# Whole weight splits, issued five steps ahead, and a recurrence that needs no paired PSUM bank

## The chip, the cores and the metric

The kernel runs on one core of one Trainium2 chip. A core has a matrix engine (TensorE, PE in the profile), VectorE (DVE), ScalarE (ACT), GpSimd (POOL) and DMA queues, here issued by SyncE (SP). Each engine works through its own list of instructions in order, and engines wait for each other on semaphores. The time is the device time of one execution, in microseconds (us), as the median of several runs.

## The reference

Two layers are applied to x of 256 tokens by 2048 channels. Each layer normalises x, multiplies it by one combined input projection, runs two groups of heads and adds an output projection. Cut to what matters:

```python
for l in range(DEPTH):                                   # DEPTH = 2
    proj = rms_norm(x, norm_g[l]) @ w_in[l]              # 2048 -> IN_COLS
    rw_in, g_rw, q, k_at, v_at, g_at = split(proj)
    r, k, v, xw, xa = split(bidir_token_shift(rw_in, shift_mu[l]))
    y_rw = rwkv7_branch(r, k, v, xw, xa, ...)            # 16 heads of 64, both directions:
    #   S = S * w_t - (S kk_t) (a_t kk_t)^T + v_t k_t^T ;  y_t = S r_t
    y_at = window_attention(rope(q), rope(k_at), v_at, sink[l])
    x = x + concat(y_rw * silu(g_rw), y_at * silu(g_at)) @ w_out[l]
out = rms_norm(x, final_g)
```

## The kernel before

**Weights.** All weights arrive in halves of 128 x 1024 f32 (512 KB), 280 of them, in three buffers `raw`. Each is split into two tiles: `hi`, a copy rounded by ACT (L215), and `lo = raw - hi` by DVE (L216), in two buffers each. `wsplit` does that in two parts of 512 columns: `hi` part, `lo` part, `hi` part, `lo` part. A half of the weights is then used in eight *steps* of three matmuls of 128 x 256 (L273 `hi` by `XH`, L274 `hi` by `XL`, L275 `lo` by `XH`), which add up in a PSUM bank `pm`. In the output projections the operands are called `MH` and `ML`.

**Order.** `Stream` hands out the steps. It issues the load and the split of the next half as soon as no more than PREFETCH steps of the present one are left (2 before). `window` runs 64 steps in 14 slots, and ahead of each slot's steps it lets generators continue up to their next `yield`. PE's instructions stand exactly in the order of the program; those of the other engines are put in order by a scheduler with priorities, by default the order of the program, with 95 places of preference for `scan_b`.

**The scan.** The recurrent heads go in eight pairs, both directions at once, in four chunks of 64 tokens. Pair p is prepared by `scan_p` in window p+1 (slots in STAGE_P); `scan_i` inverts the chunks' triangular matrices in window p+2 (STAGE_I, its last pieces in slots 0 and 1 of the window after); `scan_b` runs the recurrence over the chunks in window p+3 (STAGE_B, its tail in window p+4). So in windows 4 to 8 of each layer three pairs are in work at once; after window 9 come windows with the last scans and attention, then the output projection, which is matmuls of weights alone.

**Names.** In `scan_i`: `pg` and `ge` are the chunks' products and their masked copy (DVE L724, once for each direction), `AB` a 16-bit copy of a part (ACT L733), `pt` transpositions that ACT copies to `bt` (L754) and, by four copies, to `suv` (L759). `pq`, `pd`, `tv`, `tt` belong to the doubling of the inverse: matmuls L803 and L813 into `pq`, L819 and L821 into `pd`, casts L822 and L823. Its last steps are `pf` (L829 adds a negated identity NEYE times `tv`), `q` (ACT L836), `pn` (L840) and `vf = 2 tt + pn` (DVE L842). In `scan_b`, for each chunk: `r` (L866, in bank `pcc`, or `py` in the first chunk), copied to `rh` by ACT (L869, L872); `pu = vf rh` (L885), copied to `suv` (L890); the state in `pcc` (L888, L895) scaled into the next `suv` (DVE L897); outputs in `py` (L877, L902). Its tail is the last transposition, L922 into `pyt`, with ACT `t` (L924), DVE `t` and `mf` (L925, L614), ACT `MH` (L615) and DVE `ML` (L616).

**PSUM.** `ps_main` holds two banks for `pm`, `ps_c` one bank each for `pcc` and `py`, and `ps_w` two slots of two banks, the paired banks, in which `pg`, `pt`, `pq`, `pd`, `pf`, `pn`, `pu`, `pyt` and others take turns (`wpair`, `wbank`). A matmul into a new tile waits until the last reader of the slot's older tile is done.

Of the kernel before, what the change touches and what calls it, by code (L numbers as in the profile page):

```python
# [21 lines left out]
T = 256  # L22
# [22 lines left out]
STAGE_P = [4, 6, 7, 8, 9, 10, 11, 13]  # L45
STAGE_I = (list(range(SLOTS)), [0, 1])
STAGE_B = (list(range(1, 14)), [3])
# [6 lines left out]
PREFETCH = 2  # L54
# [74 lines left out]
def hybrid_trunk_kernel(ctx, tc, xT, wi, wv, wo, par, fing, dup, iup, sink, pos, cst, out):  # L129
# [21 lines left out]
    def wbank(name):  # L151
        return wpair(name)[:, 0]
# [52 lines left out]
    def wload(src):  # L205
        raw = wrp.tile([128, 1024], F32, tag="raw", name="raw")
        SY.dma_start(out=raw, in_=src)
        return raw

    def wsplit(raw):  # L210
        hi = wsp.tile([128, 1024], F32R, tag="hi", name="hi")
        lo = wsp.tile([128, 1024], F32R, tag="lo", name="lo")
        for i in range(2):
            q = slice(i * 512, (i + 1) * 512)
            A.activation(hi[:, q], raw[:, q], AF.Copy)  # L215
            V.tensor_tensor(lo[:, q], raw[:, q], hi[:, q].bitcast(F32), op=ALU.subtract)  # L216
        return hi, lo

    def halves(src, first=None):
        return [lambda: wsplit(first if first is not None else wload(src[0])), lambda: wsplit(wload(src[1]))]  # L220
# [78 lines left out]
    EYE, NEYE = (cp.tile([128, 64], F16, name=n) for n in ("EYE", "NEYE"))  # L299
# [6 lines left out]
    def setup():  # L306
# [49 lines left out]
        V.tensor_scalar(NEYE, EYE, -1.0, None, op0=ALU.mult)  # L356
        yield
# [248 lines left out]
    def layer(l):  # L606
# [24 lines left out]
        def scan_p(p, t):  # L631
# [21 lines left out]
            pk = wbank("pk")  # L653
            head_sums(pk, sq)
# [3 lines left out]
            for x in (LW[:, 0:T], LW[:, T : 2 * T][:, ::-1]):  # L658
                V.tensor_tensor_scan(x, msk, x, 0.0, op0=ALU.mult, op1=ALU.add)  # L659
            PP = st("pp", [2, NC, 64])  # L660
# [47 lines left out]
        def scan_i(p, t):  # L708
# [129 lines left out]
            pn = wbank("pn")  # L838
            for d, c, h in dch:
                PE.matmul(pn[half[h ^ d], d * T + c * 64 : d * T + (c + 1) * 64], hx(FN, d, c, h), hx(TT, d, c, h), start=True, stop=True)  # L840
            VF = st("vf", [2, NC * 64])
            V.scalar_tensor_tensor(  # L842
                VF.rearrange("p d x -> p (d x)"), TT.rearrange("p d c j -> p (d c j)"), 2.0, pn, op0=ALU.mult, op1=ALU.add
            )
# [3 lines left out]
        def scan_b(p, t):  # L848
# [3 lines left out]
            pc = ps_c.tile([128, 512], F32, tag="c", name="pcc")  # L852
            pS = pc[:, 0:128].rearrange("p (d j) -> p d j", d=2)
            pyt = ps_c.tile([128, 512], F32, tag="y", name="py")
            py = pyt[:, 0:256].rearrange("p (c j) -> p c j", j=64)
            for i in range(NC):
# [3 lines left out]

                pr = [pc[:, 128:192], pc[:, 192:256] if i else pyt[:, 256:320]]
                for d in range(2):
                    for h in range(2):

                        r = half[1 - h] if i == 0 else every
                        PE.matmul(pr[d][half[h ^ d]], GE[h][r, d, ci[d], 0, :], SUV[r, d, ci[d], h, :], start=True, stop=True)  # L866
                RH = st("rh", [2, 64], bufs=2)
                if i:
                    A.activation(RH, pc[:, 128:256].rearrange("p (d j) -> p d j", d=2), AF.Copy)  # L869
                else:  # L870
                    for d in range(2):
                        A.activation(RH[:, d, :], pr[d], AF.Copy)  # L872
# [8 lines left out]
                pu = wpair("pu")  # L881
                for d in range(2):
                    for h in range(2):
                        x = half[h ^ d]
                        PE.matmul(pu[half[h], d, 0:64], t["VF"][x, d, cs(ci[d])], RH[x, d, :], start=True, stop=True)  # L885
# [3 lines left out]
                for h in range(2):  # L889
                    A.activation(here(h), pu[half[h], :, 0:64], AF.Copy)  # L890
# [28 lines left out]
            pz = wbank("pyt")  # L919
# [4 lines left out]
            A.activation(Zt, pz[:, 0:T], AF.Identity, scale=prm(P_LG, p), bias=prm(P_LB, p))  # L924
# [220 lines left out]
```

## Time and profile before

| | |
|---|---|
| median of 3 runs | 1244.04 us (1242.3 to 1247.03) |
| profiled execution, its own time | 1247.3 us |
| its span | 1245.5 us |
| PE busy | 1184.3 us (95%), 16140 matmuls |
| DVE busy | 937.5 us (75%) |
| ACT busy | 739.9 us (59%) |
| DMA queue of the loads | 164.27 MB, 38.5% of 16 engines' span |
| mean granted PE clock | 0.987 |

Of the 16140 matmuls 6720 are those of the weights. A line of a timeline reads: start, duration, engine, line of the kernel, operation, output and input, shape, count, and in brackets the idle time ahead of it with what ended it. Groups by form give total busy time, the mean of one in ns, and the idle time ahead. Matmuls overlap, so what one costs is read from start to start.

### The profile page before, as it was taken

To read this page: it belongs to the slowest core of one execution; us is meant where nothing else is said; L and a number is where in the kernel's file an instruction comes from. 1 tells how busy PE (TensorE), PEld (TensorE's weight loads), DVE (VectorE), ACT (ScalarE), POOL (GpSimd) and SP (SyncE) were. 2 spreads that over 40 slices of the span, in tenths; PEclk is the share of its full clock that TensorE was granted. 3 is DMA by queue.
4 is the path that set the end of the run, shared out by engine and by line. 5 is a ranking of instruction groups with operands and counts; after the bars stand their busy time and mean duration, and the time that the engine had idled before them with its cause. 6 is when DMAs were issued, how large, how long until landed. Compare 5 with 4: busy or idle time off the path is not lost.

```text
span 1245.5 us, 38032 instructions
## 1 busy us (share of the span) xinstructions
PE 1184.3 (95%) x16140; PEld 1092.3 (88%) x16140; DVE 937.5 (75%) x2082; ACT 739.9 (59%) x1838; POOL 19.0 (2%) x23
## 2 busy tenths in 40 slices
PE   6989999999998999999999999999999989999996
PEld 6978888888887989989998888888888888899996
DVE  6878878887976678856666888878887766786654
ACT  6646665766565466645555656665766555675553
POOL 0000000000000000000000000000000000000000
PEclk9999999999999999999999999999999999999998
DMA  7443233322322434466554433233223324435653
GB/s 246 156 143 122 88 116 109 105 93 94 134 77 93 133 109 142 140 204 224 210 182 143 143 110 119 93 111 109 104 93 100 112 99 131 140 130 174 212 190 119
DMA packets 60410, 166.70 MB, mean 134 GB/s; under 512 B 7728, under 2 KB 22736, under 8 KB 60240
## 3 DMA queue, kind: packets, MB, share of 16 engines
q1 hardware_dynamic: 60240, 164.27, 38.5%
q8 instruction: 126, 2.06, 0.7%
q14 instruction: 44, 0.36, 0.1%
HBM read 157.43 MB, written 4.19 MB: 130 GB/s over the span
## 4 chain that ended last, share of the span: by engine, by line
PE 48%; DVE 18%; issue 16%; ACT 11%; DMA 4%; SPq 1%; POOL 0%; DVEq 0%; POOLq 0%; ACTq 0%
PE pm L273 13%; PE pm L275 11%; PE pm L274 11%; DVE lo L216 3%; DMA g<-dup 3%; PE pg L718 2%; DVE kd L665 2%; ACT hi L215 2%; DVE ge L724 2%; ACT AB L733 2%; ACT suv L759 2%; DVE lw L659 2%; ACT ge L771 1%; DMA rrot<-u 1%; ACT bt L754 1%
## 5 line engine op out<-in xcount | busy, mean ns | idle before, releaser
L273 PE MATMUL pm<-XH,hi 128*128 128x256 f32 x1664 | 498.1, 299 | 14.5 <-ACT XH L178 6.1
L275 PE MATMUL pm<-XH,lo 128*128 128x256 f32 x1664 | 471.4, 283 | 11.2 <-DVE lo L216 11.2
L274 PE MATMUL pm<-XL,hi 128*128 128x256 f32 x1664 | 470.6, 283 | 0.1
L215 ACT ACTIVATE hi<-raw 128x512 fp32r<-128x512 f32 x560 | 329.6, 625 | 212.1 <-PE pm L274 170.0
L216 DVE TENSOR_TENSOR lo<-raw,hi 128x512 fp32r<-128x512 f32 x560 | 369.0, 687 | 84.0 <-ACT hi L215 76.7
L273 PEld LDWEIGHTS pm<-XH,hi 128*128 128x128 f32 x1664 | 316.5, 190 | 40.2 <-issue 13.0
L275 PEld LDWEIGHTS pm<-XH,lo 128*128 128x128 f32 x1664 | 316.8, 190 | 14.6 <-DVE lo L216 14.4
L274 PEld LDWEIGHTS pm<-XL,hi 128*128 128x128 f32 x1664 | 317.3, 191 | 0.8 <-DVE XL L179 0.8
L273 PE MATMUL pm<-MH,hi 128*128 128x256 f32 x512 | 145.5, 284 | 2.3 <-ACT hi L215 2.3
L275 PE MATMUL pm<-MH,lo 128*128 128x256 f32 x512 | 145.2, 284 | 0.1
L274 PE MATMUL pm<-ML,hi 128*128 128x256 f32 x512 | 145.0, 283 | 0.0
L273 PEld LDWEIGHTS pm<-MH,hi 128*128 128x128 f32 x512 | 97.9, 191 | 3.2 <-ACT hi L215 2.5
L275 PEld LDWEIGHTS pm<-MH,lo 128*128 128x128 f32 x512 | 97.8, 191 | 0.4 <-DVE lo L216 0.4
L274 PEld LDWEIGHTS pm<-ML,hi 128*128 128x128 f32 x512 | 98.0, 191 | 0.0
L890 ACT ACTIVATE suv<-pu 64x128 f32<-64x128 f32 x128 | 34.5, 270 | 24.8 <-PE pcc L888 13.6
L724 DVE TENSOR_TENSOR ge<-pg,C 128x1024 f32<-128x1024 f32 x32 | 39.1, 1221 | 3.5 <-PE pg L718 3.5
L970 ACT ACTIVATE mv<-mv,mx 128x257 f32<-128x257 f32 x64 | 31.9, 504 | 15.9 <-DVE mx L967 15.9
L733 ACT ACTIVATE AB<-ge 64x512 f16<-64x512 f32 x32 | 20.2, 630 | 34.3 <-DVE ge L724 33.9
L718 PE MATMUL pg<-mv,bk 64*128 64x128 f32 x512 | 37.2, 285 | 0.0
L822 DVE CAST_PREDICATED tv<-LV,pd 128x256 f16<-128x256 uint8 x80 | 34.0, 426 | 4.1 <-PE pd L821 3.7
L815 ACT ACTIVATE QF<-pq 128x256 f16<-128x256 f32 x80 | 30.8, 385 | 6.8 <-PE pq L813 5.5
L823 DVE CAST_PREDICATED tt<-LV,pd 128x256 f16<-128x256 uint8 x80 | 34.0, 425 | 0.0
(241 smaller groups left out, 1833.7 us busy)
## 6 DMA issues: line engine op xcount, KB each, us to landing
raw<-wi SPq DMA_DIRECT2D x207, 512.0 KB, 3.8
raw<-wo SPq DMA_DIRECT2D x64, 512.0 KB, 3.8
raw<-wv SPq DMA_DIRECT2D x8, 512.0 KB, 3.6
rrot<-u SPq DMA_DIRECT2D x80, 32.0 KB, 2.3
vg<-xT SPq DMA_DIRECT2D x16, 128.0 KB, 3.6
xd<-vg SPq DMA_DIRECT2D x16, 128.0 KB, 3.6
vg<-xd SPq DMA_DIRECT2D x16, 128.0 KB, 3.5
g<-dup SPq DMA_DIRECT2D x16, 97.0 KB
```

What stands on the lines that cost most here:

```text
L215: A.activation(hi[:, q], raw[:, q], AF.Copy)
L216: V.tensor_tensor(lo[:, q], raw[:, q], hi[:, q].bitcast(F32), op=ALU.subtract)
L273: PE.matmul(pm, wh, rh[:, kk, :], start=(kk == 0), stop=False)
L274: PE.matmul(pm, wh, rl[:, kk, :], start=False, stop=False)
L275: PE.matmul(pm, wl, rh[:, kk, :], start=False, stop=(kk == 15))
L718: PE.matmul(pg[:, h, c * 128 : (c + 1) * 128], BK[half[h], d, c, 1 - h : 3 - h, :].rearrange("p s j -> p (s j)"), MV[half[h], d, c].rearra ...
L724: V.tensor_tensor(GEd(d), pg.rearrange("p h (c x) -> p h c x", c=NC), gm[d].unsqueeze(1).unsqueeze(1).to_broadcast([128, 2, NC, 128]), op= ...
L733: A.activation(flat(AB[half[h]]), GE[h][half[h]].rearrange("p d c s j -> p (d c) s j")[:, :, 0, :], AF.Copy)
L822: V.copy_predicated(t_sub(TC), t_mask, flat4(pd[:, :, 0:128]))
L823: V.copy_predicated(v_sub(TT), v_mask, flat4(pd[:, 0, 128:384].rearrange("p (d x) -> p d x", d=2)))
L890: A.activation(here(h), pu[half[h], :, 0:64], AF.Copy)
L970: A.activation(Sc[:, h, q, 0:257], Sc[:, h, q, 0:257], AF.Exp, scale=0.125, bias=mx[:, q : q + 1], accum_out=den[:, q : q + 1])
```

## The change

Five things are edited. (1) `wsplit` makes one `hi` and one `lo` of 1024 columns; the very first weight keeps two parts. (2) PREFETCH goes from 2 to 5 steps. (3) STAGE_P gets slot 5, with a further `yield`, so that `pk` is written a slot after the scans of `lw`; the tail of STAGE_B moves from slot 3 to slot 1. (4) The term `2 tt` is added on PE, by four matmuls per pair with EYE2, twice the identity, into `pn`, which becomes a paired bank; ACT copies it to `vf`. Rows are arranged so that `vf` has its input and output on the same half of the partitions. (5) In the recurrence `r`, `u` and the state lie in one bank `pcc`, taken anew for each chunk, so that `pu` takes no paired bank and `rh` is one copy in every chunk; the last transposition goes into the free half of `py`'s bank.

```diff
--- before.py
+++ after.py
@@ -42,16 +42,16 @@
 
 
 SLOTS = 14
-STAGE_P = [4, 6, 7, 8, 9, 10, 11, 13]
+STAGE_P = [4, 5, 6, 7, 8, 9, 10, 11, 13]
 STAGE_I = (list(range(SLOTS)), [0, 1])
-STAGE_B = (list(range(1, 14)), [3])
+STAGE_B = (list(range(1, 14)), [1])
 ATT = [
     [4, 11],
     [1, 3, 6, 8, 11, 13],
     [0, 2, 5, 7, 8, 10, 12, 13],
 ]
 PRIO_B = 95
-PREFETCH = 2
+PREFETCH = 5
 
 
 def _layout():
@@ -207,17 +207,17 @@
         SY.dma_start(out=raw, in_=src)
         return raw
 
-    def wsplit(raw):
+    def wsplit(raw, parts=1):
         hi = wsp.tile([128, 1024], F32R, tag="hi", name="hi")
         lo = wsp.tile([128, 1024], F32R, tag="lo", name="lo")
-        for i in range(2):
-            q = slice(i * 512, (i + 1) * 512)
+        for i in range(parts):
+            q = slice(i * 1024 // parts, (i + 1) * 1024 // parts)
             A.activation(hi[:, q], raw[:, q], AF.Copy)
             V.tensor_tensor(lo[:, q], raw[:, q], hi[:, q].bitcast(F32), op=ALU.subtract)
         return hi, lo
 
     def halves(src, first=None):
-        return [lambda: wsplit(first if first is not None else wload(src[0])), lambda: wsplit(wload(src[1]))]
+        return [lambda: wsplit(first, 2) if first is not None else wsplit(wload(src[0])), lambda: wsplit(wload(src[1]))]
 
     class Stream:
 
@@ -296,7 +296,7 @@
     LV = cp.tile([128, NL, 2, 128], U8, name="LV")
     AB, AL, QF = (cp.tile([128, 2, NC, 64], F16, name=n) for n in ("AB", "AL", "QF"))
     MSK = cp.tile([128, NC, 64], F16, name="MSK")
-    EYE, NEYE = (cp.tile([128, 64], F16, name=n) for n in ("EYE", "NEYE"))
+    EYE, NEYE, EYE2 = (cp.tile([128, 64], F16, name=n) for n in ("EYE", "NEYE", "EYE2"))
     band = cp.tile([128, 512], BF16, name="band")
     FG = cp.tile([128, NKT], F32, name="FG")
     SK = cp.tile([128, DEPTH * 16], F32, name="SK")
@@ -354,6 +354,7 @@
         V.tensor_copy(band, cin[:, 0:512])
         V.tensor_copy(EYE, cin[:, 512 + 64 * NL : 576 + 64 * NL])
         V.tensor_scalar(NEYE, EYE, -1.0, None, op0=ALU.mult)
+        V.tensor_scalar(EYE2, EYE, 2.0, None, op0=ALU.mult)
         yield
 
     def window(n, *gens, groups=SLOTS):
@@ -650,13 +651,14 @@
             KR = st("kkr", [T])
             A.activation(KR, K, AF.Identity, scale=prm(P_KK, p))
             yield
-            pk = wbank("pk")
-            head_sums(pk, sq)
 
             V.tensor_scalar(LW, LW, 1.0, None, op0=ALU.add)
             msk = MSK.rearrange("p c j -> p (c j)")
             for x in (LW[:, 0:T], LW[:, T : 2 * T][:, ::-1]):
                 V.tensor_tensor_scan(x, msk, x, 0.0, op0=ALU.mult, op1=ALU.add)
+            yield
+            pk = wbank("pk")
+            head_sums(pk, sq)
             PP = st("pp", [2, NC, 64])
             IP = st("ip", [2, NC, 64])
             A.activation(PP.rearrange("p d c j -> p (d c j)"), LW, AF.Exp, scale=DECAY_C)
@@ -835,13 +837,17 @@
             FN = st("q16", [2, NC, 64], F16)
             A.activation(FN.rearrange("p d c j -> p d (c j)"), pf[:, :, 0:T], AF.Copy)
             yield
-            pn = wbank("pn")
+
+            pn = wpair("pn")
+            for d in range(2):
+                for h in range(2):
+                    PE.matmul(
+                        pn[half[h], d, 0:T], EYE2[half[h ^ d]], TT[half[h ^ d], d].rearrange("p c j -> p (c j)"), start=True, stop=False, skip_group_check=True
+                    )
             for d, c, h in dch:
-                PE.matmul(pn[half[h ^ d], d * T + c * 64 : d * T + (c + 1) * 64], hx(FN, d, c, h), hx(TT, d, c, h), start=True, stop=True)
+                PE.matmul(pn[half[h], d, cs(c)], hx(FN, d, c, h), hx(TT, d, c, h), start=False, stop=True, skip_group_check=True)
             VF = st("vf", [2, NC * 64])
-            V.scalar_tensor_tensor(
-                VF.rearrange("p d x -> p (d x)"), TT.rearrange("p d c j -> p (d c j)"), 2.0, pn, op0=ALU.mult, op1=ALU.add
-            )
+            A.activation(VF, pn[:, :, 0:T], AF.Copy)
             t["VF"] = VF
             yield
 
@@ -849,27 +855,21 @@
             GE, MV, BT, SUV, PC, bv = (t[n] for n in ("GE", "MV", "BT", "SUV", "PC", "bv"))
 
 
-            pc = ps_c.tile([128, 512], F32, tag="c", name="pcc")
-            pS = pc[:, 0:128].rearrange("p (d j) -> p d j", d=2)
             pyt = ps_c.tile([128, 512], F32, tag="y", name="py")
             py = pyt[:, 0:256].rearrange("p (c j) -> p c j", j=64)
             for i in range(NC):
                 ci = [order[d][i] for d in range(2)]
 
                 here = lambda h, i=i: pick(SUV, half[h], i * 128 + h * 64, [NC * 128 + (NC - 1 - 2 * i) * 128, 2], [1, 64])
-
-                pr = [pc[:, 128:192], pc[:, 192:256] if i else pyt[:, 256:320]]
+                pc = ps_c.tile([128, 3, 2, 64], F32, tag="c", name="pcc")
+                pS = pc[:, 2]
                 for d in range(2):
                     for h in range(2):
 
                         r = half[1 - h] if i == 0 else every
-                        PE.matmul(pr[d][half[h ^ d]], GE[h][r, d, ci[d], 0, :], SUV[r, d, ci[d], h, :], start=True, stop=True)
+                        PE.matmul(pc[half[h], 0, d, :], GE[h][r, d, ci[d], 0, :], SUV[r, d, ci[d], h, :], start=True, stop=True)
                 RH = st("rh", [2, 64], bufs=2)
-                if i:
-                    A.activation(RH, pc[:, 128:256].rearrange("p (d j) -> p d j", d=2), AF.Copy)
-                else:
-                    for d in range(2):
-                        A.activation(RH[:, d, :], pr[d], AF.Copy)
+                A.activation(RH, pc[:, 0], AF.Copy)
                 yield
                 if i > 0:
                     for d in range(2):
@@ -878,16 +878,14 @@
                                 py[half[h], ci[d], :], MV[half[h], d, ci[d], 1, :], SUV[half[h], d, ci[d], h, :],
                                 start=False, stop=False, skip_group_check=True,
                             )
-                pu = wpair("pu")
                 for d in range(2):
                     for h in range(2):
-                        x = half[h ^ d]
-                        PE.matmul(pu[half[h], d, 0:64], t["VF"][x, d, cs(ci[d])], RH[x, d, :], start=True, stop=True)
+                        PE.matmul(pc[half[h], 1, d, :], t["VF"][half[h], d, cs(ci[d])], RH[half[h], d, :], start=True, stop=True)
                 if 0 < i < NC - 1:
                     for h in range(2):
                         PE.matmul(pS[half[h]], ident[half[h], half[h]], here(h), start=True, stop=False, skip_group_check=True)
                 for h in range(2):
-                    A.activation(here(h), pu[half[h], :, 0:64], AF.Copy)
+                    A.activation(here(h), pc[half[h], 1], AF.Copy)
                 yield
                 if i < NC - 1:
                     for d in range(2):
@@ -916,12 +914,12 @@
             yield
             V.tensor_tensor(ysq, py, yv.unsqueeze(2).to_broadcast([128, NC, 64]), op=ALU.mult)
             yield
-            pz = wbank("pyt")
+            pz = pyt[:, T : 2 * T]
             for c in range(NC):
                 for h in range(2):
                     PE.matmul(pz[half[h], cs(c)], ysq[half[h], c, :], ident[half[h], half[h]], start=True, stop=True)
             Zt = st("t1", [T], bufs=3)
-            A.activation(Zt, pz[:, 0:T], AF.Identity, scale=prm(P_LG, p), bias=prm(P_LB, p))
+            A.activation(Zt, pz, AF.Identity, scale=prm(P_LG, p), bias=prm(P_LB, p))
             V.tensor_tensor(Zt, Zt, bv, op=ALU.add)
             mix_split(p, Zt, t["gr"])
             yield
```

The first place is ACT in a steady window, from the last copy of one pair's inverse to the copies of `pt` (slots 0 to 3). Before:

```order
L836 ACTIVATE q_4431<-pf 128x512
L872 ACTIVATE rh<-pcc 128x64
L872 ACTIVATE rh<-py 128x64
L733 ACTIVATE AB<-ge 64x512 x2
L890 ACTIVATE suv<-pu 64x2x64 x2
L771 ACTIVATE ge<-mv 64x6x64
L215 ACTIVATE hi<-raw 128x512
L754 ACTIVATE bt<-pt 128x768
L759 ACTIVATE suv<-pt 64x4x64 x4
L771 ACTIVATE ge<-mv 64x6x64
L924 ACTIVATE t_4588<-pyt,PR 128x256
```

and with the change, in which lines have moved by a few (L922 is `t`, L850 `vf`, L735 `AB`, L888 `suv`, L756 `bt`, L761 the four copies):

```order
L838 ACTIVATE q_4333<-pf 128x512
L922 ACTIVATE t_4377<-py,PR 128x256
L650 ACTIVATE t_4599<-kr,PR 128x256
L850 ACTIVATE vf<-pn 128x512
L872 ACTIVATE rh<-pcc 128x128
L616 ACTIVATE MH<-mf 128x256
L735 ACTIVATE AB<-ge 64x512 x2
L888 ACTIVATE suv<-pcc 64x2x64 x2
L773 ACTIVATE ge<-mv 64x6x64
L215 ACTIVATE hi<-raw 128x1024
L756 ACTIVATE bt<-pt 128x768
L761 ACTIVATE suv<-pt 64x4x64 x4
```

`t` of the tail, `vf` and `MH` now stand ahead of `AB`; `t` stood behind the four copies. There is one `rh` for two.

The second place is DVE in the same stretch. Before:

```order
L724 TENSOR_TENSOR ge<-pg,C 128x2x512
L842 SCALAR_TENSOR_TENSOR vf<-tt,pn 128x512
L784 COPY tt<-EYE 128x512
L724 TENSOR_TENSOR ge<-pg,C 128x2x512
L764 TENSOR_TENSOR AL<-ge,AB 64x512 x2
L808 COPY_PREDICATED tt<-LV,AB 128x128
L216 TENSOR_TENSOR lo<-raw,hi 128x512
L897 TENSOR_TENSOR suv<-pcc,pc 64x2x64 x2
L925 TENSOR_TENSOR t_4588<-t_4588,bv 128x256
L806 COPY_PREDICATED tv<-LV,pq 128x2x128
L614 SCALAR_TENSOR_TENSOR mf<-t_4588,vg 128x256
L809 COPY_PREDICATED tt<-LV,pq 128x128
```

and with the change (L726 is `ge`, L923 `t`, L895 `suv`):

```order
L726 TENSOR_TENSOR ge<-pg,C 128x2x512
L923 TENSOR_TENSOR t_4377<-t_4377,bv 128x256
L786 COPY tt<-EYE 128x512
L615 SCALAR_TENSOR_TENSOR mf<-t_4377,vg 128x256
L617 TENSOR_TENSOR ML<-mf,MH 128x256
L726 TENSOR_TENSOR ge<-pg,C 128x2x512
L766 TENSOR_TENSOR AL<-ge,AB 64x512 x2
L810 COPY_PREDICATED tt<-LV,AB 128x128
L216 TENSOR_TENSOR lo<-raw,hi 128x1024
L895 TENSOR_TENSOR suv<-pcc,pc 64x2x64 x2
L808 COPY_PREDICATED tv<-LV,pq 128x2x128
```

`vf` is gone from DVE; `t`, `mf` and `ML` of the tail stand between the two `ge`.

The third place is DVE around the reciprocal of `kd`, in the middle of the window. Before:

```order
L216 TENSOR_TENSOR lo<-raw,hi 128x512 x2
L897 TENSOR_TENSOR suv<-pcc,pc 64x2x64 x2
L684 TENSOR_TENSOR lw<-lw,kr 128x512
L665 RECIPROCAL kd<-pk 128x256
L399 TENSOR_TENSOR u<-pm,rb 128x256
L666 SCALAR_TENSOR_TENSOR kd<-kd,kkr 128x256
L822 COPY_PREDICATED tv<-LV,pd 128x2x32x4
L401 SCALAR_TENSOR_TENSOR vg<-u,PR,vg 128x255
L823 COPY_PREDICATED tt<-LV,pd 128x2x32x4
L402 SCALAR_TENSOR_TENSOR vg<-u,PR,vg 128x255
```

and with the change (L667 is the reciprocal, L824 and L825 the casts), at the same place:

```order
L686 TENSOR_TENSOR lw<-lw,kr 128x512
L895 TENSOR_TENSOR suv<-pcc,pc 64x2x64 x2
L216 TENSOR_TENSOR lo<-raw,hi 128x1024
L667 RECIPROCAL kd<-pk 128x256
L400 TENSOR_TENSOR u<-pm,rb 128x256
L668 SCALAR_TENSOR_TENSOR kd<-kd,kkr 128x256
L824 COPY_PREDICATED tv<-LV,pd 128x2x32x4
L402 SCALAR_TENSOR_TENSOR vg<-u,PR,vg 128x255
L825 COPY_PREDICATED tt<-LV,pd 128x2x32x4
L403 SCALAR_TENSOR_TENSOR vg<-u,PR,vg 128x255
```

`lw` (L684, now L686) and `suv` stood behind the two parts of `lo`, and stand ahead of the whole one; the order from the reciprocal to the casts is the same.

## The prediction

> **What bounds the kernel now.** I read the page's first part.
>
> ```profile
> PE 1184.3 (95%) x16140; PEld 1092.3 (88%) x16140; DVE 937.5 (75%) x2082; ACT 739.9 (59%) x1838; POOL 19.0 (2%) x23
> ```
>
> TensorE (PE) is busy 95% of the span of 1245.5 us. An edit pays only if PE waits less or works less; time saved on VectorE (DVE) or ScalarE (ACT) pays only where PE is waiting for it. So the next view is PE's waits. The columns are total us, number, longest.
>
> ```profile
> PE pq L803 <- ACT suv L759: 11.6, 12, 1.5
> PE pm L275 <- DVE lo L216: 11.2, 15, 1.6
> ...
> PE pt L741 <- DVE ge L724: 3.0, 2, 1.7
> ...
> PE pf L829 <- DVE tt L823: 1.6, 2, 1.0
> ...
> PE pq L813 <- DVE tv L822: 1.5, 5, 0.4
> PE pq L813 <- DVE tt L823: 0.9, 4, 0.3
> ```
>
> The scan windows in the middle of each layer repeat, so one of the layer's five stands for ten; the columns are the window, its length and the busy time of PE, the weight loads, DVE, ACT and POOL.
>
> ```profile
> 300.32:343.18 42.86, 41.85 (x751) 37.69 (x752) 35.89 (x76) 27.84 (x73) 1.01 (x1) 1.00 0.30 103
> ```
>
> PE is busy 41.85 of 42.86 us. Its one large gap stands at slot 3; in PE's timeline and ACT's, of the window two before this one:
>
> ```profile
> 219.09 0.68 PE L922 MATMUL pyt<-C,ysq 64*64 64x64 f32 x16
> 219.71 0.45 PE L895 MATMUL pcc<-suv,bt 128*64 128x64 f32 x8
> ...
> 221.25 0.33 PE L803 MATMUL pq<-tv,AB 64*64 64x32 f16 x11 [0.86 <-ACT suv L759]
> ```
>
> ```profile
> 215.86 1.28 ACT L733 ACTIVATE AB<-ge 64x512 f16<-64x512 f32 x2 [2.10 <-DVE ge L724]
> 217.17 0.56 ACT L890 ACTIVATE suv<-pu 64x128 f32<-64x128 f32 x2
> 217.75 0.53 ACT L771 ACTIVATE ge<-mv 64x384 f32<-64x384 f32 x1
> ...
> 218.82 0.81 ACT L754 ACTIVATE bt<-pt 128x768 f32<-128x768 f32 x1
> 219.65 1.55 ACT L759 ACTIVATE suv<-pt 64x256 f32<-64x256 f32 x4
> ```
>
> `pq` needs a slot of the paired banks. There are two: `pyt` of L922 has just taken one, and `pt` holds the other until ACT has emptied it, at 221.20.
>
> **The slot-3 wait.** In the change `pu` and `pyt` take no slot, so `pq` goes into one that is free, and the four `suv` copies are next needed by the `pq` of slot 4 (L813 before). The ten steady waits and the two of window 9 make up the 11.6 us row; I count 8.6 in the steady windows (10 x 0.86).
>
> What is late next: the last transposition with its tail (ACT `t`, DVE `t` and `mf`, ACT `MH`, DVE `ML`) now stands at slot 1 ahead of the second `ge` on DVE and of `AB` on ACT, and `vf` goes from DVE to ACT. I replay the queues with rows of the same stretch.
>
> ```profile
> 212.88 0.34 PE L840 MATMUL pn<-tt,q 64*64 64x64 f16 x10
> ```
>
> ```profile
> 213.37 0.69 DVE L842 SCALAR_TENSOR_TENSOR vf<-tt,pn 128x512 f32<-128x512 f16 x1
> ...
> 214.60 1.23 DVE L724 TENSOR_TENSOR ge<-pg,C 128x1024 f32<-128x1024 f32 x1 [0.22 <-PE pg L718]
> ```
>
> ```profile
> L1043 DVE TENSOR_TENSOR mv<-mv 128x1024 f32<-128x1024 f32 x3 | 3.7, 1222 | 0.0
> ...
> L1042 ACT ACTIVATE mv<-X 128x1024 f32<-128x1024 f32 x3 | 3.0, 1048 | 0.0
> ...
> L836 ACT ACTIVATE q<-pf 128x512 f16<-128x512 f32 x16 | 9.3, 580 | 0.3 <-PE pf L834 0.3
> ```
>
> The transposition (0.62) then stands at slot 1, whose first matmul starts at 212.88; ACT is through with `t`, `kr`, `vf` (0.58, from L836), `rh` and `MH` at about 215.8, DVE with `ML` at 216.2, and the second `ge` ends near 217.5 instead of 215.83. `AB` (1.28) then ends at 218.8, `suv` (0.56) at 219.3, a whole `hi` (1.05) at 220.9, its `lo` (1.22) at 222.1, `bt` and the four copies (0.81 and 1.55) at 223.3. PE wants that `suv` at 219.9 (L895, moved by the matmuls added below), the `lo` at 222.3 and the slot of the copies at 223.3 once the gap is closed. All three just hold, so I take the full 8.6 us, and note that the last two have no more than 0.2 us to spare.
>
> **Window 9**, where the scans run out, has in each layer a wait of `pt` for `ge` (3.0 in all), of `pq` (the other 3.0 of 11.6) and of `pf` (1.6). `pt` no longer queues for the slot that `ge` empties, but for the one of `pn`; the same late `ge` is then wanted by `pq` further down. Of 7.6 us I take 5.8, most of it, since the scans' own work is thin there and DVE has gaps for it.
>
> **Slot 8 and beyond.** The waits of L813 (2.4) come from the casts of `tv` and `tt`, queued on DVE behind the reciprocal of `kd`; ahead of that DVE waits for a `hi`:
>
> ```profile
> 230.97 1.30 DVE L216 TENSOR_TENSOR lo<-raw,hi 128x512 fp32r<-128x512 f32 x2 [0.29 <-ACT hi L215]
> ```
>
> In the change `lw` and `suv` stand ahead of this `lo` and fill those 0.29 us, and a whole `lo` is 0.08 shorter, so the casts come some 0.37 earlier; the longest of these waits is 0.4. I take 1.6 of the 2.4, since an earlier PE wants them earlier too.
>
> **The wide splits.** Cost of one half of the weights:
>
> ```profile
> L215 ACT ACTIVATE hi<-raw 128x512 fp32r<-128x512 f32 x560 | 329.6, 625 | 212.1 <-PE pm L274 170.0
> L216 DVE TENSOR_TENSOR lo<-raw,hi 128x512 fp32r<-128x512 f32 x560 | 369.0, 687 | 84.0 <-ACT hi L215 76.7
> ```
>
> ```profile
> 1180.63 1.16 ACT L215 ACTIVATE hi<-raw 128x512 fp32r<-128x512 f32 x2 [1.69 <-PE pm L274]
> ...
> 1181.30 1.30 DVE L216 TENSOR_TENSOR lo<-raw,hi 128x512 fp32r<-128x512 f32 x2
> ```
>
> Two halves back to back take 1.16 and 1.30 us, one whole 1.05 and 1.22 by L1042 and L1043: 279 splits save 31 us of ACT and 22 us of DVE. PE hides both today, so I book nothing. The price is delay: the first usable `lo` comes 1.05 + 1.22 = 2.27 us after the start, where it came after some 1.30 (0.63 and 0.69). Against it stands an issue three steps, or nine matmuls of 0.119 us = 1.07 us, earlier. Where VectorE's queue made `lo` late, that helps; where the buffer or the data came late, nothing does:
>
> ```profile
> 112.13 0.38 PE L275 MATMUL pm<-XH,lo 128*128 128x256 f32 x1 [0.84 <-DVE lo L216]
> ...
> 465.11 0.39 PE L275 MATMUL pm<-XH,lo 128*128 128x256 f32 x1 [0.99 <-DVE lo L216]
> ...
> 555.40 0.58 PE L273 MATMUL pm<-MH,hi 128*128 128x256 f32 x1 [2.27 <-ACT hi L215]
> ```
>
> Four waits of the first kind in windows 2 and 3 (112.13, 153.21 and their twins in layer 2, 3.3 us) shrink by 2.0. The attention waits at 465.11 and its twin grow by the longer `lo`, 0.53 each (1.1), and 555.40, where `hi` stands behind a transfer, by 0.4 for `hi` and 0.4 for `lo` (0.8). Bounds for all splits: a gain of the whole 11.2 row, or the loss that I give to the second rival.
>
> **Matmuls added.** Four of 64x256 per pair for the sum on PE:
>
> ```profile
> 209.68 0.30 PE L829 MATMUL pf<-tv,NEYE 64*64 64x256 f16 x4
> 209.81 0.20 PE L833 MATMUL pf<-tv,AB 64*64 64x64 f16 x4
> ```
>
> The same shape takes 0.13 us to the next start, so 16 pairs cost 2.1 us. The eight `vf` matmuls of an iteration go from four tiles of the array to two (output rows equal input rows). Here `py` is on the two diagonal tiles and `pu` on all four:
>
> ```profile
> 184.40 0.39 PE L877 MATMUL py<-suv,mv 64*64 64x64 f32 x6
> 184.58 0.27 PE L885 MATMUL pu<-rh,vf 64*64 64x64 f32 x2
> ...
> 184.80 0.28 PE L888 MATMUL pcc<-suv,C 64*64 64x128 f32 x2
> ```
>
> Sixteen take 0.40 us to L888. Sixteen on diagonal tiles alone (L922) take some 0.46 before the next may start, so an iteration costs 0.06 to 0.08 more; 64 iterations at 0.07 make 4.5 us. Bounds: nothing if the neighbours fill the gaps, and 8.6 if half of L922's whole 0.62 less L741's 0.35 (216.61 to 216.95 in the next rows) is lost each time.
>
> ```profile
> 216.44 0.34 PE L885 MATMUL pu<-rh,vf 64*64 64x64 f32 x8
> 216.61 0.41 PE L741 MATMUL pt<-C,vg 64*64 64x64 f32 x16
> 216.95 0.58 PE L749 MATMUL pt<-C,bk 64*128 64x64 f32 x12
> ```
>
> The Trainium skill speaks against this edit: "TensorEngine Tiling (Array Packing)", Key Properties, says that different tiles can load weights and multiply in parallel, so two tiles take twice as long as four. L741 on four tiles at 0.34 against L922 on two at 0.62 agree. Taken strictly, a group alone (0.17 us, 216.44 to 216.61) would cost 0.17 more, 64 groups 10.9 us, and the sum below would end at 1240.9; the interleaved rows decide for 4.5.
>
> One `rh` copy for two in the first iteration, and 16 x 0.69 us of `vf` off DVE, are hidden by PE and booked at nothing; without that cover they are worth 0.2 and 0.7 us per window.
>
> **Sum.** 8.6 + 5.8 + 1.6 + 2.0 = 18.0 gained; 2.1 + 4.5 + 1.1 + 0.8 = 8.5 lost; 9.5 us net. The profiled execution took 1247.3 (span and 1.8 us around it), so 1237.8 by it. The median shown is 1244.04, 3.3 lower, and gives **1234.5 us**.
>
> **Rivals.** *The wait only moves.* The late `ge`, `AB`, `suv`, `hi` chain misses its three appointments by 0.5 us: 14 scan windows x 0.5 = 7.0 back, 1241.5. For it: 0.2 us of room in my replay. Against it: ACT is busy 27.84 of 42.86 us, and the order could only be late, not short of capacity.
>
> *Slower: wide splits starve PE.* The place is each half's first L275. In 60 of the 280 halves the second part of `lo` was not ready when that matmul ran; today it has four more steps. In a steady window:
>
> ```profile
> 223.04 0.28 PE L275 MATMUL pm<-XH,lo 128*128 128x256 f32 x1
> ```
>
> ```profile
> 223.70 0.69 DVE L216 TENSOR_TENSOR lo<-raw,hi 128x512 fp32r<-128x512 f32 x1
> ```
>
> The matmul at 223.04 precedes the end of `lo`, 224.39, by 1.35. Such deficits, taken half by half (the largest 3.02), add up to 52 us; if the earlier issue brings only 0.8 us of its 1.07, 17.0 us are left. Then 1234.5 + 17.0 = 1251.5. It is slower by 0.5% from a lead under some 0.8 us. For it: two buffers of `hi`, for which ACT waits 170.0 us. Against it: those waits are early, and in the output projections `lo` comes about 1 us ahead.
>
> *More goes than I book.* With 53 us less on ACT and DVE, all of the 11.6, 3.0, 2.4 and 1.6 and half of the 11.2 vanish: 24.2, less 6.6 of added matmuls, is 17.6, so 1226.4.
>
> **Chances.** Forecast 0.45, wait moves 0.25, slower 0.12, more 0.18. A measurement of this kernel cannot tell less than 0.5% (6.2 us) from no change, so faster means under 1237.8. That holds for most of the forecast's case (0.40 of 0.45), all of the last and little of the second: faster 0.60, same 0.29, slower 0.11. The forecast's own range is 1229 to 1240; with the other cases and the unknown prices 1223 to 1249.
>
> **What would show it.** Right: no wait of `pq` for the copies of `pt`, steady windows of 42.0 to 42.3 us, the second `ge` ending some 1.6 us later after slot 1's start, L813's successor without its gap at slot 8, `vf` groups 0.07 us longer. Wrong: PE waits of a like size at the recurrence's `suv`, at L275 in steady windows (first or second rival), or a gap at slot 4 for the copies. The forecast fails if the steady windows stay within 0.2 us of 42.86.

## The result, and the profile after

The changed kernel takes 1260.06 us (median of 4 runs, 1258.39 to 1262.97) where the kernel before, on the same chip, takes 1245.53 (1242.3 to 1247.57): a ratio of 1.012 with a 95% interval of 1.0096 to 1.0143. It is slower; 1234.5 was forecast, with 1249 as the upper end of the wider range.

The first part of the page after:

```profile
PE 1197.2 (95%) x16204; PEld 1104.1 (88%) x16204; DVE 908.8 (72%) x1788; ACT 720.4 (57%) x1559; POOL 19.3 (2%) x23
```

DVE and ACT work less, by 28.7 and 19.5 us, and the span is 15.7 us longer. (PE's "busy" grew by 12.9 us, but this is not all work: the row of a window below has 42.58 us of it, and the same window without waits, shown with the order held, 42.10.) PE's waits after:

```profile
PE pm L275 <- DVE lo L216: 11.4, 15, 1.8
PE pq L815 <- DVE tv L824: 9.4, 18, 1.8
PE pcc L893 <- ACT suv L888: 7.5, 12, 1.4
PE pm L273 <- ACT hi L215: 6.3, 4, 2.1
```

The row of 11.6 us of `pq` for the copies of `pt` is gone. In its place stand 9.4 us for `tv` (2.4 for `tv` and `tt` before) and 7.5 us for ACT's `suv`, a wait that did not exist.

Where the 15.7 us lie follows from the start of the inverse's last product (L829 before, L831 after) in each window, and from the last product of the attention (differences of unrounded times):

| stretch | before | after | difference |
|---|---|---|---|
| start to window 3 of layer 1 | 124.0 | 121.1 | -2.8 |
| five scan windows, layer 1 | 214.2 | 218.1 | +3.9 |
| the next two | 89.4 | 88.6 | -0.8 |
| attention, layer 1 | 105.1 | 108.3 | +3.2 |
| output projection, layer 2 to window 3 | 201.4 | 202.2 | +0.8 |
| five scan windows, layer 2 | 214.2 | 218.1 | +3.9 |
| the next two | 87.7 | 92.2 | +4.5 |
| attention, layer 2 | 104.3 | 107.8 | +3.5 |
| last output projection | 105.3 | 104.7 | -0.5 |

Of each five scan windows the first is unchanged and four, called steady here, are longer by 0.98 us each. One of these after, with its length and the busy time of PE, weight loads, DVE, ACT, POOL:

```profile
251.55:295.40 43.85, 42.58 (x755) 38.40 (x754) 34.75 (x66) 27.51 (x66) 1.01 (x1) 1.00 0.33 103
```

**The slot-3 gap closed.** PE's timeline after, at slot 3:

```profile
261.62 0.45 PE L893 MATMUL pcc<-suv,bt 128*64 128x64 f32 x8
261.90 0.40 PE L900 MATMUL py<-suv,ge 128*64 128x64 f32 x8
262.23 0.33 PE L805 MATMUL pq<-tv,AB 64*64 64x32 f16 x10
```

From L900 to `pq` it is 0.33 us, where 219.99 to 221.25 before was 1.26.

**A new wait two slots later.** ACT before, then ACT after, then PE after, around the second chunk's `suv`:

```profile
269.49 0.82 ACT L647 ACTIVATE th<-pza,DP 128x256 f32<-128x256 f32 x2
270.94 0.57 ACT L890 ACTIVATE suv<-pu 64x128 f32<-64x128 f32 x2 [0.63 <-PE pcc L888]
272.12 0.63 ACT L662 ACTIVATE pp<-lw 128x512 f32<-128x512 f32 x1 [0.61 <-DVE lw L659]
```

```profile
268.48 0.83 ACT L648 ACTIVATE th<-pza,DP 128x256 f32<-128x256 f32 x2
270.92 0.63 ACT L664 ACTIVATE pp<-lw 128x512 f32<-128x512 f32 x1 [1.60 <-DVE lw L658]
271.46 0.54 ACT L888 ACTIVATE suv<-pcc 64x128 f32<-64x128 f32 x2
```

```profile
268.52 0.40 PE L883 MATMUL pcc<-rh,vf 64*64 64x64 f32 x8
...
272.05 0.45 PE L893 MATMUL pcc<-suv,bt 128*64 128x64 f32 x8 [0.59 <-ACT suv L888]
```

`u` is in PSUM shortly after 268.9. ACT could copy it from 269.3 on, but the exponential `pp` now stands ahead of `suv` in ACT's list and waits 1.60 us for DVE's scans of `lw`. Before, `suv` stood first. PE waits 0.59 us; its gap is 0.66 longer than the 0.21 of such a change-over.

The late `pp` has a second price. On DVE the two products `mv` that read it stand ahead of the casts of `tv` and `tt`, which stood ahead of them before (272.01 and 272.33 against 272.79). DVE after and PE after:

```profile
271.59 0.42 DVE L675 SCALAR_TENSOR_TENSOR mv<-pp,kkr 128x252 f32<-128x252 f32 x1 [0.70 <-ACT pp L664]
...
272.25 0.44 DVE L824 CAST_PREDICATED tv<-LV,pd 128x256 f16<-128x256 uint8 x1
272.59 0.44 DVE L825 CAST_PREDICATED tt<-LV,pd 128x256 f16<-128x256 uint8 x1
```

```profile
272.75 0.30 PE L815 MATMUL pq<-tv,AB 64*64 64x32 f16 x16
273.17 0.65 PE L629 MATMUL pk<-t,C 64*64 64x256 f32 x4
```

`pq` starts when the cast of `tv` is done, and `pk` follows it after 0.42 us, where it followed after 0.15 before (273.79 and 273.94). Beyond the delay of `suv` itself these two starts come 0.37 us late in a window, and no row of the waits shows it in full (0.12 is recorded at `pk`).

**And one at slot 9.** DVE after and PE after:

```profile
238.91 0.58 DVE L895 TENSOR_TENSOR suv<-pcc,pc 64x128 f32<-64x128 f32 x2
239.52 1.23 DVE L216 TENSOR_TENSOR lo<-raw,hi 128x1024 fp32r<-128x1024 f32 x1
240.77 0.42 DVE L824 CAST_PREDICATED tv<-LV,pd 128x256 f16<-128x256 uint8 x1
```

```profile
240.27 0.45 PE L870 MATMUL pcc<-suv,ge 128*64 128x64 f32 x8
241.25 0.30 PE L815 MATMUL pq<-tv,AB 64*64 64x32 f16 x16 [0.53 <-DVE tv L824]
```

A whole `lo`, issued five steps ahead, stands ahead of the casts, and PE's `pq` waits 0.53 us for them. In the kernel before the two parts of that `lo` came behind the casts and nothing waited.

### The profile page after: what moved, and what is told of

It is laid out like the page before. It is cut to its first block, busy times and chain, and to the rows that moved or that the text cites. A ratio compares the mean times of both kernels' runs of the same rounds, so it can differ in the third digit from the quotient of the medians.

```text
span 1261.2 us, 37601 instructions
## 1 busy us (share of the span) xinstructions
PE 1197.2 (95%) x16204; PEld 1104.1 (88%) x16204; DVE 908.8 (72%) x1788; ACT 720.4 (57%) x1559; POOL 19.3 (2%) x23
## 5 line engine op out<-in xcount | busy, mean ns | idle before, releaser
L273 PE MATMUL pm<-XH,hi 128*128 128x256 f32 x1664 | 498.8, 300 | 13.2 <-ACT XH L178 5.7
L275 PE MATMUL pm<-XH,lo 128*128 128x256 f32 x1664 | 473.9, 285 | 11.3 <-DVE lo L216 10.7
L216 DVE TENSOR_TENSOR lo<-raw,hi 128x1024 fp32r<-128x1024 f32 (+1 forms) x281 | 342.5, 1219 | 146.7 <-ACT hi L215 144.9
L215 ACT ACTIVATE hi<-raw 128x1024 fp32r<-128x1024 f32 (+1 forms) x281 | 296.3, 1055 | 220.1 <-PE pm L274 174.8
L275 PEld LDWEIGHTS pm<-XH,lo 128*128 128x128 f32 x1664 | 317.9, 191 | 18.1 <-DVE lo L216 18.0
L275 PE MATMUL pm<-MH,lo 128*128 128x256 f32 x512 | 145.5, 284 | 0.8 <-DVE lo L216 0.8
L275 PEld LDWEIGHTS pm<-MH,lo 128*128 128x128 f32 x512 | 98.4, 192 | 1.0 <-DVE lo L216 1.0
L888 ACT ACTIVATE suv<-pcc 64x128 f32<-64x128 f32 x128 | 34.4, 269 | 19.7 <-PE pq L815 13.7
L726 DVE TENSOR_TENSOR ge<-pg,C 128x1024 f32<-128x1024 f32 x32 | 39.0, 1217 | 2.4 <-PE pg L720 2.1
L735 ACT ACTIVATE AB<-ge 64x512 f16<-64x512 f32 x32 | 20.1, 629 | 31.6 <-DVE ge L726 31.2
L824 DVE CAST_PREDICATED tv<-LV,pd 128x256 f16<-128x256 uint8 x80 | 34.1, 427 | 1.9 <-PE pd L823 1.4
L815 PE MATMUL pq<-tv,AB 64*64 64x32 f16 x1280 | 26.0, 184 | 9.6 <-DVE tv L824 9.4
```

The costliest lines, as they stand in the source:

```text
L273: PE.matmul(pm, wh, rh[:, kk, :], start=(kk == 0), stop=False)
L275: PE.matmul(pm, wl, rh[:, kk, :], start=False, stop=(kk == 15))
L726: V.tensor_tensor(GEd(d), pg.rearrange("p h (c x) -> p h c x", c=NC), gm[d].unsqueeze(1).unsqueeze(1).to_broadcast([128, 2, NC, 128]), op= ...
L815: PE.matmul(narrow(pq[:, d], h ^ d, c), hq(AB, d, c, h), sub(TC, h, d, c, d * b), start=True, stop=True)
L824: V.copy_predicated(t_sub(TC), t_mask, flat4(pd[:, :, 0:128]))
L888: A.activation(here(h), pc[half[h], 1], AF.Copy)
```

## The experiments

All ratios are against the kernel before, runs on the same chip.

**One part alone, and one part undone.** First the split part alone, in the kernel before:

```diff
-PREFETCH = 2
+PREFETCH = 5
-        for i in range(2):
-            q = slice(i * 512, (i + 1) * 512)
+        for i in range(parts):          # parts = 1; 2 for the first weight
+            q = slice(i * 1024 // parts, (i + 1) * 1024 // parts)
```

> The kernel before with only the weight-split part of the change: whole splits of 1024 columns, issued five steps ahead; PSUM, slots and inverse as before. Theory S (whole splits put one 1.22 us subtraction, and an exponential that waits, ahead of short links of the recurrence and the inverse on VectorE and ScalarE, and in the attention windows bring the first lo later): the 0.9 us slot-3 wait stays, about 0.6 and 0.66 us are added per steady window and 8 us in the attention windows, so 1258 to 1266 us, 1 to 1.6% slower than before. Theory P (the cost is in the PSUM part: matmuls added on TensorE and the moved tail): 1240 to 1248 us, no change.

1263.33 us, ratio 1.0148 (1.0117 to 1.0178): in theory S's range, but the waits are in part others than S named:

```profile
PE pq L803 <- ACT t L924: 17.3, 12, 2.0
PE pq L813 <- DVE tv L822: 5.2, 16, 1.3
```

`pp` stands ahead of `suv` here too, yet PE has no row of waiting for ACT's `suv`. Instead the slot-3 wait has grown (1.33 us at 221.40, 0.86 before). Scan windows are 44.0 us.

The PSUM part alone is the changed kernel with

```diff
-    def wsplit(raw, parts=1):
+    def wsplit(raw, parts=2):
-PREFETCH = 5
+PREFETCH = 2
-STAGE_P = [4, 5, 6, 7, 8, 9, 10, 11, 13]      # and its yield ahead of pk
+STAGE_P = [4, 6, 7, 8, 9, 10, 11, 13]
```

> The kernel before with only the PSUM part of the change: recurrence and last transposition out of the paired banks, tail at slot 1, inverse summed on TensorE; splits in two parts of 512 columns two steps ahead and the preparation's slots as before. Theory S: the slot-3 wait of 0.9 us goes, about 0.3 us per scan window of matmuls is added, a part of the new wait for suv behind the exponential stays: 1238 to 1246 us. Theory P: most of the loss of the change shows here, 1253 to 1260 us.

1254.46 us, 1.0068 (1.0049 to 1.0087): outside what theory S allowed, and within what P expected. Its rows of waits show that the added matmuls, one half of P, are not the loss:

```profile
PE pm L275 <- DVE lo L216: 21.5, 28, 1.6
PE pcc L892 <- ACT suv L887: 11.0, 11, 2.3
```

Here too `pp` stands ahead of `suv`, though splits and the slots of the preparation are those of before, and in a steady window PE waits 0.85 us for `suv` and 0.81 for `lo`. So either part of the change disturbs the order; whether the moved tail, the other half of P, or another edit of this part does it is not shown. A third theory was needed, O: the time was lost by places in the order of ACT and DVE, the two of `suv` and `tv` above all.

The early issue undone (`PREFETCH = 2` in the changed kernel):

> The changed kernel with splits issued two steps ahead as before, but whole. Theory S (the size of the split is what harms): as slow as the changed kernel or slower, 1258 to 1268 us, since the first lo of a half comes later still. Theory F (the earlier issue harms, because it puts the subtraction ahead of other work): the order of before comes back and the time with it, 1244 to 1250 us.

1263.9 us, 1.0132 (1.0098 to 1.0166). F falls: the earlier issue is not what harms whole splits. It does choose who waits: scan windows are as long as the changed kernel's (43.84), but in a steady window PE waits at one L275 for `lo` (0.61 us at 240.06) and no longer for the casts of slot 9.

```profile
PE pm L275 <- DVE lo L216: 19.5, 30, 1.5
```

The whole splits undone (`parts=2` in the changed kernel):

> The changed kernel with splits in two parts of 512 columns, still issued five steps ahead. Theory S: the attention windows get their 8 us back and the casts at slot 9 wait for 0.69 us less of subtraction: 1240 to 1250 us. Theory F: no change against the changed kernel, 1256 to 1262 us.

1246.82 us, 1.0006 (0.9993 to 1.0019). As S expected in size, but only in part by its reasons. The attention came back (104.6 and 105.4 us). The casts at slot 9 are still waited for (0.48 us, 0.53 in the changed kernel), scan windows are 43.77 us, hardly shorter than the changed kernel's 43.84, and the wait for `suv` stayed:

```profile
PE pcc L893 <- ACT suv L888: 10.9, 11, 2.6
```

Of the 17.8 us between the two profiled executions 8.7 lie in one stretch, from the output projection of layer 1 to window 3 of layer 2. There the granted clock was at half for 10.2 us in the changed kernel's execution and never in this one (more on this in the last section), so not all of the 13 us is waiting saved.

The early issue of parts alone, in the kernel before (`PREFETCH = 5`):

> The kernel before with the issue five steps ahead and nothing else. If the earlier issue of parts helps by itself (the parts of 512 columns come earlier and are short enough to pass between other work): 1236 to 1242 us. If it is neutral and the difference between the PSUM part alone and the changed kernel in parts came from elsewhere: 1243 to 1248 us.

1245.44 us, 0.9998 (0.9984 to 1.0013): neutral. In its steady windows `suv` had stayed ahead of `pp`.

**The order held.** To put `suv` first without another change, the exponentials get a dependence on it:

```diff
+    Z0 = cp.tile([128, 1], F32, name="Z0")
+    V.memset(Z0, 0.0)
                 for h in range(2):
                     A.activation(here(h), pc[half[h], 1], AF.Copy)
+                if i == 1:
+                    A.activation(Z0[half[1]], pick(SUV, half[1], i * 128 + 64, [1, 1]), AF.Copy, scale=0.0)
-            A.activation(PP..., LW, AF.Exp, scale=DECAY_C)
-            A.activation(IP..., LW, AF.Exp, scale=-DECAY_C)
+            A.activation(PP..., LW, AF.Exp, scale=DECAY_C, bias=Z0)
+            A.activation(IP..., LW, AF.Exp, scale=-DECAY_C, bias=Z0)
```

In the changed kernel:

> The changed kernel with one addition: the two exponentials (pp, ip) take a zero bias that is written after the copy of u into suv of the second chunk, so that on ScalarE suv stands ahead of them; on VectorE the casts of slot 9 then also stand ahead of the whole lo. Theory O (the steady windows lose by these two places in the order): the waits of 0.66 us for suv and of 0.6 us for tv go in the ten steady windows, 1246 to 1251 us, while the attention windows stay slow. Theory P (matmuls added on TensorE and the moved tail): no change against the changed kernel, 1256 to 1262 us.

1239.26 us, 0.9951 (0.9933 to 0.9969): 20.8 us faster than the changed kernel, more than expected. ACT, DVE and a window of it:

```profile
265.71 0.56 ACT L890 ACTIVATE suv<-pcc 64x128 f32<-64x128 f32 x2
266.30 0.20 ACT L892 ACTIVATE Z<-suv 64x1 f32<-64x1 f32 x1
267.50 0.72 ACT L666 ACTIVATE pp<-lw,Z 128x512 f32<-128x512 f32 x1 [1.00 <-DVE lw L660]
```

```profile
235.95 0.58 DVE L899 TENSOR_TENSOR suv<-pcc,pc 64x128 f32<-64x128 f32 x2
237.29 0.42 DVE L826 CAST_PREDICATED tv<-LV,pd 128x256 f16<-128x256 uint8 x1
237.62 0.42 DVE L827 CAST_PREDICATED tt<-LV,pd 128x256 f16<-128x256 uint8 x1
237.96 1.22 DVE L216 TENSOR_TENSOR lo<-raw,hi 128x1024 fp32r<-128x1024 f32 x1
```

```profile
206.00:248.10 42.10, 42.10 (x759) 38.16 (x758) 34.59 (x66) 27.80 (x67) 1.01 (x1) 1.00 0.34 107
```

`suv` is first, the casts are ahead of the whole `lo`, and PE is busy 42.10 of 42.10 us: no wait is left in a scan window. It is also the length that the prediction gave. Laid side by side matmul by matmul, a window of the changed kernel falls behind this one by 0.65 us at `suv`, 0.37 at the `pq` and `pk` behind the casts of slot 5, 0.17 at an L275, and 0.53 at the casts of slot 9: 1.72 in all, which is the difference in length (43.84 and 42.11). The ten scan windows together hold 15.9 of the 24.6 us between the two profiled executions. One edit moved all these places, so whether each pays by itself is not told by this run.

The control, the same bias in the kernel before:

> The kernel before with the zero bias alone. There suv stands ahead of the exponentials already. Theory O (the zero bias pays only by holding an order that the change lost): 1240 to 1247 us, no difference that can be told. If the bias speeds the scan up by itself: 1228 to 1238 us, and the gains with it say nothing on the change.

1238.52 us, 0.995 (0.9934 to 0.9966), between the two answers: the bias also pays 7 us here. Its steady windows, where `suv` was first already, are 42.6 us, only 0.25 shorter. The first scan window of each layer is 41.3, 1.6 shorter, and there the kernel before has `pp` ahead of `suv` as well:

```profile
142.22 0.63 ACT L662 ACTIVATE pp<-lw 128x512 f32<-128x512 f32 x1 [1.52 <-DVE lw L659]
142.76 0.55 ACT L890 ACTIVATE suv<-pu 64x128 f32<-64x128 f32 x2
```

So most of what the control gains in its scan windows (3.2 of 5.0 us) is an order held, too. It also fits that the change left the first of each five windows as long as it was: it had the costly order already. The wait of `pq` for the copies of `pt` is as before:

```profile
PE pq L805 <- ACT suv L761: 11.7, 12, 1.6
```

So of the 20.8 us some 14 (20.8 - 7.1, medians) are what the change had lost by the order beyond what the kernel before loses by it; counted in the scan windows alone it is 15.9 less 5.0, or 11. This is an estimate, since it takes the bias to be worth the same in both. Against this control the changed kernel with the order held is the same (1239.26 and 1238.52).

The split part with the bias, PSUM as before:

> The kernel before with the whole splits five steps ahead and the zero bias, PSUM as before. If the steady windows lost by the order alone, the split part that cost 17 us without the bias (1263) comes to 1248 to 1254 us: the attention windows stay 8 us slower, the slot-3 wait stays. If whole splits starve TensorE in the steady windows too: 1256 to 1264 us.

1254.34 us, 1.0077 (1.0056 to 1.0097), just above the first answer; 9.0 less than without the bias and 15.8 more than the control. Its steady windows are 43.27, and PE's main wait is of `pq` for the last transposition's slot of the paired banks:

```profile
PE pq L805 <- ACT t L928: 15.8, 12, 2.0
```

Whole splits make the old slot-3 wait worse (1.35 us in a steady window, 0.87 in the control); the PSUM part removes it. So whole splits need the PSUM part; the next run shows that the PSUM part does not need whole splits.

**Parts and whole.** The changed kernel in parts, with the bias:

> The changed kernel with splits in two parts of 512 columns (five steps ahead) and the same zero bias. If order and whole splits are independent causes: 1247 less 0.9 us for suv and 0.5 us for tv in ten windows, 1232 to 1238 us, faster than both kernels. If the two waits only hide another one behind them: 1243 to 1248 us.

1232.78 us, 0.9889 (0.986 to 0.9918): in the first answer's range, 14 us less than without the bias. Of the two waits only the one for `suv` went from the steady windows; the one for the casts of slot 9 stayed (0.43 us at 239.05), and the windows are 42.52 with PE busy for 42.10:

```profile
PE pq L817 <- DVE tv L826: 5.5, 14, 0.5
```

The two causes do not simply add up: the bias brings 20.8 us with whole splits and 14.0 with parts, and parts bring 13.2 us without the bias and 6.5 with it. Whole splits in the scan windows and parts in the attention windows and the output projection (the number of parts is set to 1 at each layer's start and to 2 ahead of the attention):

> The changed kernel with the zero bias, whole splits in the scan windows and two parts in the attention windows and the output projection. If the loss of the whole splits lies in the attention windows alone (steady windows 42.1 us against 42.5 in parts): 1228 to 1233 us. If it lies in the scan windows too: 1236 to 1240 us.

1232.8 us, 0.9903 (0.9886 to 0.9919): 6.5 us less than whole throughout, and the same as parts throughout, though the scan windows are 42.12 against 42.52. In the profiled executions attention takes 105.2 and 104.7 us against 108.0 and 107.3 with whole splits, which is 5.4. So the loss of whole splits, once the order holds, lies mostly there. Rows of PE after show where; the first stands beside the 0.99 at 465.11 before, and the other two matmuls did not wait before:

```profile
466.67 0.38 PE L275 MATMUL pm<-XH,lo 128*128 128x256 f32 x1 [1.48 <-DVE lo L216]
```

```profile
488.79 0.39 PE L275 MATMUL pm<-XH,lo 128*128 128x256 f32 x1 [0.44 <-DVE lo L216]
```

```profile
509.49 0.39 PE L275 MATMUL pm<-XH,lo 128*128 128x256 f32 x1 [0.29 <-DVE lo L216]
```

**Without the added matmuls.** The kernel before, with `PREFETCH = 5` and the bias as above, and of the PSUM part only the last transposition out of the paired banks:

```diff
-STAGE_B = (list(range(1, 14)), [3])
+STAGE_B = (list(range(1, 14)), [0])
-            pz = wbank("pyt")
+            pz = pyt[:, T : 2 * T]
```

> The kernel before with the last transposition in the free half of the bank of py (tail at slot 0 of the next window), issue five steps ahead in parts, and the zero bias; the recurrence keeps its paired bank, and no matmul is added. The slot-3 wait then goes without the 0.3 us of added matmuls per window: 1228 to 1236 us if the order theory holds and the paired banks needed only this one tile less; 1240 to 1248 us if pq still waits for a slot.

1231.63 us, 0.9883 (0.9856 to 0.9909), the fastest median of all, though not apart from 1232.78. The first answer's range is met, but not by its reason: `pq` no longer waits for a slot, a wait of `pg` for `ge` stands in its place (0.77 us in a steady window for 0.87), and the steady windows are no shorter than the control's (42.60 and 42.61). The 6.9 us against the control lie elsewhere, and that control issues two steps ahead, so how much of them the transposition brings is not told.

```profile
PE pg L720 <- DVE ge L726: 9.3, 12, 0.8
```

The same with whole splits in the scan windows:

> The kernel before with the last transposition in the bank of py at slot 0, the zero bias, and splits as in the run with both sizes; no matmul added. 1226 to 1232 us if its steady windows gain by whole splits as the changed kernel's do; 1232 to 1240 us if the wait for ge that this placing brings grows with them.

1234.03 us, 0.991 (0.9891 to 0.9929): no difference that can be told from the run in parts, and no gain by whole splits. The wait for `ge` did grow, as the second answer had it:

```profile
PE pg L723 <- DVE ge L729: 13.6, 14, 1.1
```

## Why the prediction was wrong

**The slot-3 wait: right.** The 11.6 us are gone. The replay of the queues, which gave the second `ge` an end 1.6 us later, was good: after slot 1's first matmul it ended 2.95 us before and 4.33 us after,

```profile
257.88 1.22 DVE L726 TENSOR_TENSOR ge<-pg,C 128x1024 f32<-128x1024 f32 x1
```

with L920 starting at 254.77, so 1.4 later. The three appointments held as forecast: PE waits for none of the three.

**The step that failed is the sum's silence on the rest of the order.** It took from the order only the three places quoted, checked the path as far as slot 4 and the reciprocal, and counted every other piece of ACT and DVE as standing where it stood. Three did not: `pp` passed `suv`, the products that read `pp` passed the casts of slot 5, and a whole `lo` passed the casts of slot 9, each on a chain with no slack: 0.65, 0.37 and 0.53 us in a window. The steady windows, forecast at 42.0 to 42.3, were 43.84. With the order held they were 42.1, so the sum for these windows was right and a term was missing. These engines run their lists in order, so the places stood in the order before the run. The prediction had a wait at the recurrence's `suv` among its signs of being wrong, and its first rival (the wait only moves) had the kind of loss right, but put it in the chain of `ge` and `AB` at slots 1 to 4, which held.

**"PE hides both today, so I book nothing" for whole splits: wrong in size.** The delay of the first `lo` was priced at 1.1 us for the attention, which lost 6.7 us (3.2 and 3.5); parts gave 5.4 of such a loss back. The term at 465.11 was right (0.53 forecast, 0.49 measured, 1.48 less 0.99), but three places a layer wait at L275 and not one: 2.2 and 2.6 us in the two layers, 1.0 in each before. Waits for ACT's `suv` and `pp` grew too, by 1.6 and 0.8 us; the rest is not placed. The second rival named this mechanism with 17 us, but put it in the steady windows, where L275 has no wait of note in the changed kernel (with the issue two steps ahead it has).

**Window 9: wrong.** 5.8 us were booked; the two windows gained 0.8 us in layer 1 and lost 4.5 in layer 2. The waits for `ge` and for the slot went, but waits in the recurrence and the inverse stand in their place, which the 5.8 us had not allowed for: in layer 1 0.98 us for ACT's `suv` (395.16) and 1.13 for DVE's (408.19), in layer 2 0.78 for DVE's (1025.80) and 1.84 at 1036.31, where `pq` waits for casts behind a rotation and a whole `lo`, after a transfer:

```profile
1032.62 0.42 DVE L496 TENSOR_TENSOR u<-u,TW 128x256 f32<-128x256 f32 x1 [4.54 <-DMA rrot<-u]
...
1034.25 1.22 DVE L216 TENSOR_TENSOR lo<-raw,hi 128x1024 fp32r<-128x1024 f32 x1
...
1035.84 0.42 DVE L824 CAST_PREDICATED tv<-LV,pd 128x256 f16<-128x256 uint8 x1
```

Most of the difference between the layers is the clock's. In these windows the granted clock was at half for 3.4 us once in layer 1 before (398.2) and twice in layer 2 after (982.4 and 1037.0). Beside the same matmuls in the other layer each such stretch costs some 1.5 us. Without them the change would have lost about 0.7 us in layer 1 and 1.5 in layer 2, an estimate, and still have gained nothing.

**The matmuls added: right.** In a window without waits PE needs 42.10 us; the window before less its waits of 0.93 and 0.29 is 41.64. The difference, 0.46, stands against 0.13 + 4 x 0.07 = 0.41 forecast. Twice the time on two tiles as on four, taken strictly, would have given 0.13 + 4 x 0.17 = 0.81; the interleaved rows were the better guide.

**Windows 2 and 3**: 2.0 us were booked for both layers. Layer 1 is 2.8 us ahead at window 3; the like stretch of layer 2, with an output projection ahead of it, is 0.8 longer. Right at most in part.

What stays open: why the scheduler placed `pp` and `lo` as it did. The orders show that either part of the change is enough for the first, and that a dependence undoes both in the changed kernel; its reasons were not tried.

## What to carry to other kernels

Where a scheduler sets the order, an edit's cost is not only what it edits: compare the lists of every engine over a whole period, and for each instruction that a short chain waits for, look at what has come to stand ahead of it and what that one waits for itself. If such a place has moved, holding it with a dependence is the first experiment, since it parts the price of the order from that of the edit; here that gave some 14 us to the order (11 by the scan windows alone) and left the change itself at no difference. A wider instruction saves time on its engine and adds delay to its first user, so look at the width stage by stage: the price stands where the user waits. Here whole splits kept to the scan windows shortened these by 0.4 us each, and the whole kernel was no faster than with parts throughout.

## What the runs showed of the hardware that was not expected

A group of matmuls can cost less where the next has its tile shape. The sixteen of the last transposition took 0.62 us to the next start before (219.09 to 219.71, to a matmul on another tile shape), of which 0.15 is the last step to that other shape, where the steps between their pairs are 0.05. After, with matmuls of the same shape behind them and interleaved with them, their own share from start to start is 0.44 us in a window. Shape and interleaving are not told apart here.

A wait of TensorE may cost more than its length. The granted clock falls to half for 3.4 us at a time, or twice that: in the changed kernel from 982.4, after PE's wait of 1.54 us at 982.26, the matmuls of the weights start 0.21 us apart, and 0.12 apart at the same place of layer 1 (365.4), where a wait of 1.54 us had stood as well and the clock stayed full. In the traces of all the runs such stretches, those at the very end aside, come during or within 3 us after a wait of 1.2 us or more, and most waits of 1.2 to 1.6 us are followed by none; no run changed such a wait alone, so that the wait brings the stretch on is not shown. Profiled executions differ by it: the changed kernel's has 23.8 us at half clock ahead of its end, that of the kernel before 20.4, that in parts (1246.82) 3.4.
